# Layer 1's modulation products: 16 of 32 move from layer 0's output projection to its second attention's keys and queries

## The chip, the cores and the metric

The kernel runs on one core of one Trainium2 chip. Its time is device microseconds of one execution, the median of several runs. A core has TensorE (PE: matrix products), VectorE (DVE), ScalarE (ACT) and GpSimd (POOL) for work on tiles, and SyncE (SP), whose queue here issues most DMAs. All engines run side by side; each takes its own instructions in order, and semaphores tie them together.

## The reference, cut to what matters

Two layers of a transformer trunk with two attention branches, for 512 latent and 256 context tokens of width 1024. Layer 1 computes latent tokens alone. Everything is float32 at the borders.

```python
def _layer(x, ctx, c, c_ctx, w_ada, b_ada, norm_g, w_in, ..., update_ctx):
    mod_x = jax.nn.silu(c) @ w_ada + b_ada                 # (3 * 1024,)
    shift_x, scale_x, gate_x = jnp.split(mod_x[:, None, :], 3, axis=-1)
    mod_c = jax.nn.silu(c_ctx) @ w_ada + b_ada
    shift_c, scale_c, gate_c = jnp.split(mod_c, 3)
    hx = _rmsnorm(x, norm_g) * (1.0 + scale_x) + shift_x
    hc = _rmsnorm(ctx, norm_g) * (1.0 + scale_c) + shift_c
    px = hx @ w_in                                         # keys, values, queries, z paths, gates
    ...
    a_att = _na_latent(qa, ka, va, cka, cva, rpb, rows)    # first attention: a 2-D window and all context
    b_att = _gqa_latent(qb, k_all, v_all)                  # second attention: 8 query heads, 2 key/value heads
    o_a = (a_att * jax.nn.silu(a_z)) @ w_o_a
    o_b = (b_att * jax.nn.silu(b_z)) @ w_o_b
    out_x = (jax.nn.sigmoid(g_a) * o_a + jax.nn.sigmoid(g_b) * o_b) @ w_out
    x_new = x + gate_x * out_x
```

The vectors `c` and `c_ctx` are known from the start, so the modulation of both layers can be computed at any time before it is used: layer 1's shift and scale are first used when its normalised rows are made, at the end of layer 0.

## The kernel before, in words

**Products on TensorE.** Each float32 product is made of three: operands are split into a high and a low half (`whi` by ScalarE, `wlo` by VectorE or GpSimd), and high x high, high x low and low x high are summed in PSUM (`mm3`, lines 435 to 437). `tok_proj` projects one tile of 128 tokens with all eight blocks of the contracted dimension; `chan_proj` projects one block of 128 output channels.

**The modulation.** Layer 0's shift and scale are products on TensorE at the start. The rest is computed on VectorE in the background: `ada_steps` gives a list of steps, to be run one by one between the pieces of other work. For one half `h` of the contracted dimension (512 of 1024), a first step (`load`, line 286) broadcasts that half of silu(c) and silu(c_ctx) to all partitions, a tile `cb` with a single buffer. Then there are, for each of the named blocks `i` of 128 output channels, two products (`dot`, line 297), one for c and one for c_ctx: a multiply-sum along 512 elements on VectorE. The first of the two also issues the load of the block's weights (`rawb`, 256 KB, line 290, two buffers), on SP's queue or on another that is named. `asum` keeps the sums, and `ada_mod(1)` makes layer 1's shift and scale (`modc`) of both halves. Blocks 0 to 15 are shift and scale, 16 to 23 the gate. `gate_steps` is the same for the gate of the layer itself.

Each product is tied by `behind(ON_DVE, ...)` to stand after the VectorE instruction that was emitted last. Otherwise a planner (the tile framework's scheduler) orders every engine's instructions before the run, in program order where its own estimate says that they are ready, and ahead of it where they are ready earlier.

**The stages of layer 0, with their background lists.**

- First value projection: layer 1's first half, blocks 0 to 15, both vectors.
- First attention (window).
- Second attention's keys and values (`load_w2(W, C_BKV, ...)`, six token tiles, lines 1110 to 1114), then its queries (six token tiles, lines 1126 to 1133): the list is `gate_steps((0,))`, 17 steps, one a tile and then two a tile. In each tile `head_rstd` sums squares (line 505, VectorE; 508, GpSimd), `rope_heads` scales and rotates (lines 517, 586, 591 on VectorE, 588 on GpSimd, the last two for latent tokens only), and `turn` transposes on TensorE (line 529), two tiles later (`hp["lag"]`). After the last tile, two pieces of the gate projection are run with the last transposes behind them, and the heads' pool is closed.
- Second attention: `gate_steps((1,))` and the rest of the gate projections and the first branch's output projection (`fill`) in the background. `prepare` splits the first branch's result in halves, with four subtractions on GpSimd (line 668).
- Merge and output projection (`w_out`, lines 1242 to 1266, two halves of the output channels with six token tiles each): the list is layer 1's second half, its weights loaded by GpSimd's queue (`G`), and `ada_mod(1)`. It is spread over the six tiles of the first half:

```python
            bg = ada_steps(1, range(16), (1,), 2, mp, G) + [lambda: ada_mod(1)] if first else []
            run(bg, 1)
            per_bg = -(-len(bg) // nt)
```

  In the second half each finished tile goes through `make_hx` (a sum of squares on ScalarE, line 330, GpSimd's power, 331 and 332, and the scaled row `y` on VectorE, 334) and `turn_hx` (transposes on TensorE, line 343, shift and scale on ScalarE, 346) into layer 1's input.

Of the kernel before, what the change touches and what calls it, by code (L numbers as in the profile page):

```python
# [52 lines left out]
def R(ap):  # L53
    return ap.bitcast(F32R)
# [18 lines left out]
def hybrid_kernel(es: ExitStack, tc, x, ctx, cvec, w_ada, w_ada0, small, gvec, w_in, w_o_a, w_o_b, w_out,  # L73
                  bias_int, bias_edge, rope, ident_d, out):
    nc = tc.nc
    V, S, G, T = nc.vector, nc.scalar, nc.gpsimd, nc.tensor
# [10 lines left out]
    def nm(s):  # L87
        uid[0] += 1
        return f"{s}_{uid[0]}"
# [188 lines left out]
    def ada_steps(l, tiles, halves, nv, pool, queue=None):  # L278

        cb = {}  # L280

        def load(h):
            cb[h] = pool.tile([128, 2, 512], F32, tag="cb", name=nm("cb"), bufs=1)
            for v in range(nv):
                src = cd[8 * v + 4 * h:8 * v + 4 * h + 4].rearrange("k p -> (k p)").unsqueeze(0)
                nc.sync.dma_start(cb[h][:, v, :], src.to_broadcast([128, 512]))

        def load_tile(h, i):
            cb["w"] = pool.tile([128, 512], F32, tag="rawb", name=nm("rawb"), bufs=2)
            (queue or nc.sync).dma_start(cb["w"], w_ada[l, h, i])  # L290

        def dot(h, i, v):
            if v == 0:
                load_tile(h, i)
            w = cb["w"]
            o = w if v == nv - 1 else pool.tile([128, 512], BF16, tag="junk", name=nm("junk"), bufs=1)
            behind(ON_DVE, lambda: V.tensor_tensor_reduce(o, w, cb[h][:, v, :], 1.0, 0.0, ALU.mult, ALU.add,
                                                          asum[:, i, h, v:v + 1]))
        res = []
        for h in halves:  # L300
            res += [lambda h=h: load(h)] + [lambda h=h, i=i, v=v: dot(h, i, v) for i in tiles for v in range(nv)]
        return res

    def ada_sum(a, b, nv):
        s = sp.tile([128, b - a, 2], F32, tag="as", name=nm("as"), bufs=1)
        V.tensor_tensor(s[:, :, 0:nv], asum[:, a:b, 0, 0:nv], asum[:, a:b, 1, 0:nv], ALU.add)
        return s

    def ada_mod(l):
        mod_finish(l, ada_sum(0, 16, 2).rearrange("p (a k) v -> p a k v", a=2), 0, 8)  # L310
# [157 lines left out]
    hp = {"late": [], "lag": 0}  # L468
# [4 lines left out]
    def behind(engine, fn, after=None):  # L473

        n = len(nc.cur_bb.bb.instructions)
        after = latest(engine, 1) if after is None else after
        fn()
        for i in nc.cur_bb.bb.instructions[n:]:
            if i.engine == engine:
                for last in after:  # L480
                    tc.add_manual_dep(i, last, mybir.DependencyInfo(
                        mybir.DependencyClass.NoSync, mybir.DependencyReason.DATA), reason="program order")
                after = [i.name]
# [6 lines left out]
    def run(fill, n):  # L490
        for _ in range(min(n, len(fill))):
            fill.pop(0)()
# [102 lines left out]
    def layer(l, hx, nxt, start):  # L595
        first = l == 0
# [7 lines left out]
        def gate_steps(halves, pool):  # L604
            return (ada_steps(l, range(16, 24), halves, nv, pool)
                    + ([lambda: ada_gate(l, nv, pool)] if 1 in halves else []))
# [100 lines left out]
        if first:  # L707
# [22 lines left out]
            bg = ada_steps(1, range(16), (0,), 2, hp["p"])  # L730
        else:
# [5 lines left out]
            bg = gate_steps((0, 1), hp["p"])  # L737
# [49 lines left out]
        if True:  # L787
# [267 lines left out]
            bg = []  # L1055
# [40 lines left out]
                halves(vf.rearrange("p t (h d) -> p (t h) d", h=2), vb.rearrange("p t h q d -> p (t h) q d"),  # L1096
                       vs[:, 0:1])

            bg = gate_steps((0,), hp["p"]) if first else []
            w = load_w2(W, C_BKV, KT, mix_lo)  # L1100
            w_q = []

# [7 lines left out]
            for t in range(6):  # L1110
                tok_proj(w, 256, a_hx, t, evac_bkv)
                if t == 2:
                    behind(ON_DVE, lambda: make_tabs(0))
                run(bg, 1)
            hp["lag"] = 2
            qbv = big("qb").rearrange("p (j n) -> p j n", j=4)
            fill = in_order(gates[n_na:] + o_chunks("a", prepare, evac_a))
# [7 lines left out]
                    rope_heads(4, ps, rs, gbc[:, 0, :], None, qbv, t)  # L1125
            for t in range(qt):
                tok_proj(w_q, 512, a_hx, t, evac_bq)
                run(bg, 2)
                if t == STAGE_T[0]:
                    split_vb()  # L1130
                if t in STAGE_T:
                    e = STAGE_T.index(t)
                    stage_k(kbv[:, 0, :], e, gkt[e][0], gkt[e][1], True)
# [66 lines left out]
            bg = gate_steps((1,), Parts(att["p"], own)) if first else []  # L1200
# [3 lines left out]
        with tc.tile_pool(name=f"mrg{l}", bufs=1, reuse_waits="tile") as mp:  # L1204
            open_ps(x=5)
            extra = lambda name: mp.tile([128, 3072], F32, tag="extra", name=nm(name))
            gv = mp.tile([128, nv, DM], F32, tag="gate", name=nm("gate"), bufs=1)
            for v in range(nv):
                src = gd[l][8 * v:8 * v + 8].rearrange("k p -> (k p)").unsqueeze(0)
                nc.sync.dma_start(gv[:, v, :], src.to_broadcast([128, DM]))  # L1210
            hilo(zb, gated["b"], [3], V, spans)
            mg = []

            def evac_b(f, n0, n1, ps):
                a, b = tg_part(0, f, n0, n1), tg_part(1, f, n0, n1)
                V.scalar_tensor_tensor(b, b, 1.0, ps, ALU.add, ALU.mult)  # L1216
                V.tensor_tensor(a, a, b, ALU.add)  # L1217
                hi, lo = [m[:, f % 4, n0:n1] for m in mg[f // 4]]
                S.copy(R(hi), a)
                V.tensor_tensor(R(lo), a, hi, ALU.subtract)  # L1220
            chunks = o_chunks("b", None, evac_b)
            chunks[0][0]()
            for i in range(4):
                if i < 3:
                    chunks[i + 1][0]()
                if i % 2 == 0:
                    mg.append(hilo_tiles("m"))
                for piece in chunks[i][1]:
                    piece()

            nt = 6 if first else 4
            xv = [a.rearrange("p (t n) -> p t n", t=3) for a in (big("xt0"), extra("xt1"))]
            xts = []
            for t in range(nt):
                xt = xv[t // 3][:, t % 3, :]
                nc.sync.dma_start(xt, x_src(t) if first else xs1[128 * t:128 * t + 128, :])
                xts.append(xt)
            a_m = lambda part, k: mg[k // 4][part][:, k % 4, :]
            bg = ada_steps(1, range(16), (1,), 2, mp, G) + [lambda: ada_mod(1)] if first else []
            run(bg, 1)  # L1240
            per_bg = -(-len(bg) // nt)
            for n in range(2):
                w = load_w(w_out[l], 512 * n, 512, KT, mix_lo)

                def evac_o(t, ps, n=n):
                    cs = slice(512 * n, 512 * n + 512)
                    t1 = mp.tile([128, 512], F32, tag="t1", name=nm("t1"), bufs=2)
                    V.tensor_tensor(t1, ps, gv[:, 0 if t < 4 else 1, cs], ALU.mult)
                    xt = xts[t]
                    V.tensor_tensor(xt[:, cs], xt[:, cs], t1, ALU.add)  # L1250
                    if not first:
                        nc.sync.dma_start(o_lat[16 * t:16 * t + 16][:, :, cs], xt[:, cs])
                    elif n == 1:
                        if t < 4:
                            G.dma_start(xs1[128 * t:128 * t + 128, :], xt)
                        late.append(lambda: make_hx(1, t, xt, nxt(), mp))
                late = []
                if first and n == 1:
                    hp["lag"] = 2
                for t in range(nt):  # L1260
                    if not first and n == 1 and t == nt - 1:
                        break
                    tok_proj(w, 512, a_m, t, evac_o)
                    run(bg, per_bg)
                    run(late, len(late))
                turn_late(0)
            if not first:

                for c0, c1 in ((0, 256), (256, 512)):
                    ws = [(hi[:, c0:c1], lo[:, c0:c1]) for hi, lo in w]  # L1270
                    cs = slice(512 + c0, 512 + c1)
                    ps = psw(c1 - c0)
                    tok_mm(ps, ws, c1 - c0, a_m, nt - 1, 0, KT)
                    t1 = mp.tile([128, 512], F32, tag="t1", name=nm("t1"), bufs=2)[:, :c1 - c0]
                    V.tensor_tensor(t1, ps, gv[:, 0, cs], ALU.mult)
                    xt = xts[nt - 1]
                    V.tensor_tensor(xt[:, cs], xt[:, cs], t1, ALU.add)
                    (nc.sync if c0 else S).dma_start(o_lat[16 * nt - 16:16 * nt][:, :, cs], xt[:, cs])
# [247 lines left out]
```

## Time and profile before

| what | value |
|---|---|
| time, median of 3 runs | 1110.77 us (1109.96 to 1110.95) |
| the profiled execution's own time | 1110.55 us |
| its span, first to last instruction | 1108.8 us |
| mean granted TensorE clock | 0.995 |
| keys, values and queries of layer 0's second attention | about 300 to 360 us |
| layer 0's second attention | about 374 to 545 us |
| layer 0's output projection | about 585 to 650 us |

In the profile's rows a line number is that of the instruction's source line, which is often a helper's. PE stands for TensorE's matrix products, PEld for its weight loads, SPq for SyncE's queue of DMAs. Ends of matrix products are modelled, so PE's busy time is an upper bound.

### The profile page before, as it was taken

The numbers are of one execution on the slowest core, as the hardware profiler recorded it, in microseconds if no ns is written. First come the engines' busy times: TensorE is split into PE (matmuls) and PEld (weight loads), VectorE is DVE, ScalarE is ACT, GpSimd is POOL, SyncE is SP. The second block draws the span as 40 slices with busy tenths as digits, with TensorE's granted clock in tenths as the row PEclk, the third lists the DMA queues.
The fourth block names the chain that finished last, engine by engine and source line by source line (L and its number), as shares of the span: only waits on it lengthen the run. The fifth ranks groups of instructions, "written<-read, shape, count | busy, mean of one in ns | idle before, by whom it ended". The sixth has DMA issues, their size and how long they took to land. (4 is left out here: it accounts for less than half of the span.)

```text
span 1108.8 us, 16943 instructions
## 1 busy us (share of the span) xinstructions
PE 1074.5 (97%) x5672; PEld 876.9 (79%) x5672; DVE 767.4 (69%) x1600; ACT 617.2 (56%) x1236; POOL 470.1 (42%) x397
## 2 busy tenths in 40 slices
PE   8999999899999999979999999999999999999998
PEld 6688888788888877757788878888877888777677
DVE  5567799974378478676577785466997665777473
ACT  6464279776333566655330275444899446786430
POOL 1044235554256244454521455232355472564531
PEclk9999999999999999989999999999999999999999
DMA  9454325554543498769533542453565536879642
GB/s 374 153 169 143 91 70 116 125 137 121 174 141 117 132 205 185 172 185 271 171 105 125 166 136 82 138 165 99 132 148 130 156 106 171 200 232 236 188 152 77
DMA packets 236001, 171.79 MB, mean 155 GB/s; under 512 B 160141, under 2 KB 201865, under 8 KB 234249
## 3 DMA queue, kind: packets, MB, share of 16 engines
q1 hardware_dynamic: 228576, 156.31, 51.7%
q0 software_dynamic: 2368, 7.87, 2.2%
q10 hardware_dynamic: 4968, 6.53, 1.8%
q8 instruction: 45, 0.74, 0.3%
q14 instruction: 44, 0.35, 0.1%
HBM read 115.58 MB, written 17.32 MB: 120 GB/s over the span
## 5 line engine op out<-in xcount | busy, mean ns | idle before, releaser
L838 POOL TENSOR_TENSOR h<-p,h 128x256 f16<-128x256 f32 (+2 forms) x104 | 113.1, 1096 | 167.7 <-ACT h L837 119.9
L422 POOL TENSOR_TENSOR wlo<-raw,whi 128x512 fp32r<-128x512 f32 x70 | 98.8, 1416 | 124.5 <-ACT whi L420 80.9
L435 PE MATMUL psf<-hx,whi 128*128 128x512 f32 (+1 forms) x360 | 137.5, 382 | 2.5 <-ACT zt L625 1.3
L437 PE MATMUL psf<-hx,wlo 128*128 128x512 f32 (+1 forms) x360 | 135.5, 376 | 0.0
L436 PE MATMUL psf<-hx,whi 128*128 128x512 f32 (+1 forms) x360 | 135.4, 376 | 0.0
L435 PE MATMUL psx<-whi,hx 128*128 128x512 f32 (+1 forms) x328 | 121.0, 372 | 0.0
L420 ACT CAST whi<-raw 128x512 fp32r<-128x512 f32 x136 | 82.9, 620 | 67.5 <-DMA raw<-in_w_in_dram 48.3
L437 PE MATMUL psx<-whi,hx 128*128 128x512 f32 (+1 forms) x328 | 120.0, 367 | 0.0
L436 PE MATMUL psx<-wlo,hx 128*128 128x512 f32 (+1 forms) x328 | 119.6, 366 | 0.0
L408 POOL TENSOR_TENSOR wlo<-raw,whi 128x512 fp32r<-128x512 f32 x40 | 59.5, 1489 | 119.2 <-ACT whi L405 76.0
L405 ACT CAST whi<-raw 128x512 fp32r<-128x512 f32 x88 | 54.2, 623 | 96.8 <-PE psx L437 34.2
L508 POOL TENSOR_TENSOR ss<-ss,ehalf 128x8 f32<-128x8 f32 (+2 forms) x40 | 63.6, 1593 | 77.8 <-DVE ss L505 72.5
L422 DVE TENSOR_TENSOR wlo<-raw,whi 128x512 fp32r<-128x512 f32 x66 | 70.8, 1073 | 35.2 <-ACT whi L420 34.1
L837 ACT CAST h<-p 128x256 f16<-128x256 f32 (+2 forms) x136 | 81.6, 616 | 7.7 <-DMA ct<-h 3.7
L435 PEld LDWEIGHTS psf<-hx,whi 128*128 128x128 f32 x360 | 67.8, 188 | 15.1 <-ACT zt L625 2.5
L1157 DVE CUSTOM_DVE_ANT_0 p<-pss,vb 128x768 f32<-128x768 f32 x64 | 60.4, 954 | 25.4 <-PE pss L887 22.7
L1158 ACT ACTIVATE p<-pss,mx 128x768 f32<-128x768 f32 x64 | 57.6, 901 | 35.7 <-DVE mx L1157 34.8
L437 PEld LDWEIGHTS psf<-hx,wlo 128*128 128x128 f32 x360 | 67.8, 188 | 11.8
L436 PEld LDWEIGHTS psf<-hx,whi 128*128 128x128 f32 x360 | 67.9, 189 | 10.7
L437 PEld LDWEIGHTS psx<-whi,hx 128*128 128x128 f32 x328 | 61.9, 189 | 10.2
L436 PEld LDWEIGHTS psx<-wlo,hx 128*128 128x128 f32 x328 | 62.0, 189 | 9.4
L435 PEld LDWEIGHTS psx<-whi,hx 128*128 128x128 f32 x328 | 61.8, 189 | 9.1 <-issue 0.2
(338 smaller groups left out, 2972.4 us busy)
## 6 DMA issues: line engine op xcount, KB each, us to landing
raw<-in_w_in_dram SPq DMA_DIRECT2D x168, 256.0 KB, 2.9
rawb<-in_w_ada_dram SPq DMA_DIRECT2D x48, 256.0 KB, 2.8
raw<-in_w_out_dram SPq DMA_DIRECT2D x32, 256.0 KB, 2.9
tg<-gs SPq DMA_DIRECT2D x4, 1536.0 KB, 7.1
rawx<-in_w_ada_dram SPq DMA_DIRECT2D x4, 1024.0 KB, 10.7
rawy<-in_w_ada_dram SPq DMA_DIRECT2D x4, 1024.0 KB, 9.3
gs<-zt ACTq DMA_DIRECT2D x16, 256.0 KB, 2.9
raw<-in_w_o_a_dram SPq DMA_DIRECT2D x16, 256.0 KB, 3.1
```

The source lines that it names most:

```text
L405: S.copy(hi[:, :n], raw[:, :n])
L408: e.tensor_tensor(lo[:, :n], raw[:, :n], F(hi[:, :n]), ALU.subtract)
L420: S.copy(hi, raw)
L422: lo_eng(i).tensor_tensor(lo, raw, F(hi), ALU.subtract)
L435: T.matmul(ps, lhs[0], rhs[0], start=first, stop=False)
L436: T.matmul(ps, lhs[0], rhs[1], start=False, stop=False)
L437: T.matmul(ps, lhs[1], rhs[0], start=False, stop=last)
L508: G.tensor_tensor(ss, ss, ehalf[:, :n], ALU.pow)
L837: S.copy(h[:, 0], p[:, :n])
L838: eng.tensor_tensor(h[:, 1], p[:, :n], h[:, 0], ALU.subtract)
L1157: V.tensor_tensor_reduce(p, pss, lift, -1.0, 3e38, ALU.add, ALU.min, mx[:, 0:1])
L1158: S.activation(p, pss, AF.Exp, bias=mx[:, 0:1], accum_out=r[:, i:i + 1])
```

## The change

The steps of layer 1's second half are cut in two lists. Blocks 0 to 7, 16 products behind a broadcast of their own, are put behind the gate's steps in the list of the second attention's keys and queries, and that list is run at twice the pace. Their weights are loaded by SP's queue. Blocks 8 to 15 and `ada_mod(1)` stay in the output projection.

```diff
-            bg = gate_steps((0,), hp["p"]) if first else []
+            bg = gate_steps((0,), hp["p"]) + ada_steps(1, range(8), (1,), 2, hp["p"]) if first else []
             w = load_w2(W, C_BKV, KT, mix_lo)
...
                 tok_proj(w, 256, a_hx, t, evac_bkv)
                 if t == 2:
                     behind(ON_DVE, lambda: make_tabs(0))
-                run(bg, 1)
+                run(bg, 2)
...
                 tok_proj(w_q, 512, a_hx, t, evac_bq)
-                run(bg, 2)
+                run(bg, 4)
...
-            bg = ada_steps(1, range(16), (1,), 2, mp, G) + [lambda: ada_mod(1)] if first else []
+            bg = ada_steps(1, range(8, 16), (1,), 2, mp, G) + [lambda: ada_mod(1)] if first else []
```

In layer 1 both lists are empty, so nothing changes there in the program.

## The prediction

> **What bounds the kernel now.** I read the page first (engine shares, slices, costly groups), then the table by stretches for the two stages that the change touches, then who waited for whom there, and last the instructions in order of time around each wait. The page's first row names the bound:
>
> ```profile
> PE 1074.5 (97%) x5672; PEld 876.9 (79%) x5672; DVE 767.4 (69%) x1600; ACT 617.2 (56%) x1236; POOL 470.1 (42%) x397
> ```
>
> Time can be won or lost only where TensorE (PE) stands still, or where its clock is not full. The table by stretches (us, then PE, PEld, DVE, ACT, POOL busy with counts, clock, DMA share, GB/s) for the second attention's keys and queries of layer 0 (300 to 360) and its output projection (585 to 645):
>
> ```profile
> 300.00:360.00 60.00, 60.00 (x349) 52.21 (x348) 44.71 (x92) 23.43 (x49) 35.08 (x27) 1.00 0.43 137
> 585.00:645.00 60.00, 58.62 (x263) 48.10 (x262) 45.09 (x103) 11.92 (x24) 19.81 (x28) 1.00 0.49 157
> 90.00:150.00 60.00, 60.00 (x302) 49.97 (x301) 48.69 (x107) 25.43 (x40) 19.05 (x11) 1.00 0.33 101
> ```
>
> PE has no idle time at all in the first and 1.4 us in the second. The third row, layer 0's first value projection, carries 32 such products and is the fullest VectorE stretch: 48.7 of 60 us, without a PE gap. The products themselves (line 297), by the same table for these instructions alone; the count holds two instructions a product, the multiply-sum and the read of its accumulator:
>
> ```profile
> 300.00:360.00 60.00, 12.24 (x30) 1.00 0.43 137
> 585.00:645.00 60.00, 22.05 (x64) 1.00 0.49 157
> ```
>
> So 15 products in the keys-and-queries stretch cost 0.82 us each, and 32 in the output projection 0.69. The difference is waiting for GpSimd (below).
>
> **What the output projection gives up, and gets.** 16 of 32 products leave, 16 x 0.69 = 11.0 us of VectorE, with 8 of 16 loads of 256 KB from POOL's queue. The only PE wait there is for the first transpose of layer 1's normalised rows (the products' group, min/median/max ns, first and last start; then rows in order of time, us, duration, in brackets the idle time before and what ended it):
>
> ```profile
> L297 DVE CUSTOM_DVE_ANT_0 junk<-rawb,cb x16: 674/688/694, 593.9 to 637.8; 128x512 bf16<-128x512 f32 x16
> ...
> 633.09 0.69 DVE L1248 TENSOR_TENSOR t<-psx,gate 128x512 f32<-128x512 f32 x1
> 633.69 0.68 DVE L297 CUSTOM_DVE_ANT_0 rawb<-rawb,cb 128x512 f32<-128x512 f32 x1
> 634.30 0.69 DVE L1250 TENSOR_TENSOR xt<-xt,t 128x512 f32<-128x512 f32 x1
> ...
> 637.82 0.69 DVE L297 CUSTOM_DVE_ANT_0 junk<-rawb,cb 128x512 bf16<-128x512 f32 x1 [0.41 <-DMA rawb<-in_w_ada_dram]
> 638.43 0.76 DVE L334 TENSOR_SCALAR y<-xt,ss 128x1024 f32<-128x1024 f32 x1
> 639.71 0.67 DVE L297 CUSTOM_DVE_ANT_0 rawb<-rawb,cb 128x512 f32<-128x512 f32 x1
> ...
> 639.25 1.09 PE L343 MATMUL pst<-ident,y 128*128 128x128 f32 x8 [1.38 <-DVE y L334]
> ```
>
> Products stand inside this chain: one between the two steps of the residual (0.61 us from start to start), one ahead of y (0.61). The first product starts at 593.9 and the last at 639.7: 16 tiles in 46 us, 2.9 each, paced by a load that waits for the products two tiles back. Eight tiles end near 593.9 + 23 = 617, so none is left at 633. The chain comes 1.2 us earlier, and the wait for a load in front of 637.82 goes too (0.4): the 1.38 us wait is gone. **Gain 1.4 us** (0 to 1.4: there is no other idle PE time in the stage). Next in line nothing is late: the modulation is ready near 620, its first reader ran at 642.8, and it feeds a PE that is busy for 20 of 20 us:
>
> ```profile
> 642.80 2.89 ACT L346 ACTIVATE half<-pst,modc 128x128 f32<-128x128 f32 x8
> 645.00:665.00 20.00, 20.00 (x104) 16.62 (x103) 17.25 (x27) 16.67 (x41) 9.70 (x11) 1.00 0.39 119
> ```
>
> POOL loses 8 issues and the waits before them; the one PE wait in 585 to 645 is not for POOL: 0.
>
> **What the keys and queries take on.** The background list grows from 17 places (a broadcast load and 16 gate products) to 34, taken two a token tile in the key/value loop and four in the query loop instead of one and two: 12 places, then 4, 4, 4, 4, 4, 2. The added broadcast is the 18th place, in the second query tile, so the 16 moved products fall into the last four and a half query tiles, and the gate products are pressed ahead of them. Added VectorE time by that stretch's own price: 16 x 0.82 = 13.1 us. The stretch would stand at 44.7 + 13.1 = 57.8 of 60, far above the fullest that runs without a PE gap (48.7).
>
> Its 15.3 idle us are not free, since most are links of the chain that makes each query tile (VectorE's waits, 290 to 375: us in total, times, longest):
>
> ```profile
> DVE ry L517 <- POOL ss L508: 8.4, 8, 1.8
> DVE rr L591 <- POOL ry L588: 2.6, 5, 1.2
> ```
>
> A product fits into such a gap only when the order of VectorE's queue puts it there; it is tied behind the last VectorE step emitted, so products of a tile lie ahead of the next tile's sum of squares. I take half of the idle time, 7.6 us, as filled. One more product than before lies behind the last tile's chain (0.8). So the last tile's rotated queries come 13.1 - 0.8 - 7.6 = 4.7 us late. How much slack they have stands in the order of time:
>
> ```profile
> 346.05 1.78 DVE L297 CUSTOM_DVE_ANT_0 rawb<-rawb,cb 128x512 f32<-128x512 f32 x1
> 347.76 1.77 DVE L297 CUSTOM_DVE_ANT_0 junk<-rawb,cb 128x512 bf16<-128x512 f32 x1
> ...
> 347.24 1.75 POOL L422 TENSOR_TENSOR wlo<-raw,whi 128x512 fp32r<-128x512 f32 x1
> ...
> 359.63 0.69 DVE L586 TENSOR_TENSOR rr<-ry,gbc 128x512 f32<-128x512 f32 x1
> 360.46 0.63 PE L529 MATMUL pst<-ident,rr 128*128 128x128 f32 x4
> 362.62 1.94 DVE L880 TENSOR_TENSOR qs<-qb,qs 64x768 fp32r<-64x768 f32 x2 [1.69 <-ACT qs L879]
> 374.08 0.40 PE L886 MATMUL pss<-gk,qs 128*128 128x512 f32 x1
> ```
>
> The queries are done at 360.32 and transposed at 360.46: slack 0.14. PE takes its queue in order, so a delay is a PE wait unless the planner, which fixed the order beforehand, puts the next gate projection ahead (24 matmuls at 58.62/263 = 0.22, 5.4 us). With that the stall is 0: after it the scores have cover, 374.08 - 364.56 = 9.5 us. **Stall 0 to 4.6 us; I take 4.0**, near the upper end, because the transposes now stand at the earliest place the program allows, and a planner does not see what waiting on GpSimd adds.
>
> That waiting is in the rows: two products took 1.78 us instead of 0.69 while GpSimd split a weight. [...] By the old place's price (0.69) the delay would be 11.0 - 0.7 - 7.6 = 2.7 us.
>
> **Queues and loads.** SP issues eight more tile loads in place of POOL, and two more broadcasts:
>
> ```profile
> rawb<-in_w_ada_dram SPq DMA_DIRECT2D x48, 256.0 KB, 2.8
> rawb<-in_w_ada_dram POOLq DMA_DIRECT2D x16, 256.0 KB, 3.1
> cb<-cd SPq DMA_DIRECT2D x8, 256.0 KB, 4.8
> SPq L290 <- DVE asum L297: 28.3, 5, 9.5
> 355.80 0.68 DVE L422 TENSOR_TENSOR wlo<-raw,whi 128x512 fp32r<-128x512 f32 x1
> 360.85 0.48 PE L435 MATMUL psx<-hx,whi 128*128 128x512 f32 x1
> ```
>
> A tile load on SP waits for the products two tiles back (9.5 us at the longest), and gate weights are queued behind it. Their last low halves are made at 355.8 and read by the projection that starts at 360.9, with k in order: some 6 us of cover. I take 0; if the cover is gone, the price is 9.5 - 6 = 3.5 us. The added broadcast has one buffer: its load waits for the last gate product, then 4.8 us to land. Behind the first moved product on VectorE lie the next tile's sum of squares and, through it, PE's transposes. Bounds 0 (the next tile's steps are ordered first) to 4.8; I take 0, since a planner that knows the load's length orders ready steps first. The bytes are moved, not added, except 0.5 MB at a DMA share of 0.43: 0. The two products of the last tile end before 374 either way: 0.
>
> **Sum.** 4.0 - 1.4 = +2.6 us. The profiled execution took 1110.55 us, 1108.8 of span and 1.75 around it, 0.22 under the median. So 1113.15 for such an execution and **1113.4** against the median of 1110.77. The case's own range: 1110.8 - 1.4 + 0 = 1109.4 to 1110.8 - 1.4 + 4.6 + 3.5 = 1117.5. The 3.5 also holds what a fall of the clock after a stall would cost (1.7, worked out below); the 1.38 us wait brought none. A measurement of this kernel can tell about 0.2%, 2.2 us, from no change.
>
> **Rivals.**
> *Faster: a blocked split in the attention falls elsewhere.* The dearest place between the two stages:
>
> ```profile
> 483.66 8.22 DVE L422 TENSOR_TENSOR wlo<-raw,whi 128x512 fp32r<-128x512 f32 x1
> 482.98 7.12 POOL L668 TENSOR_TENSOR gal<-za,gah 128x768 fp32r<-128x768 f32 x4
> PE psv L849 <- DVE ho L825: 5.8, 1, 5.8
> 490.00:495.00 5.00, 1.44 (x5) 1.25 (x6) 4.10 (x6) 0.00 (x0) 2.74 (x4) 0.65 0.53 109
> 495.00:500.00 5.00, 5.00 (x19) 3.75 (x18) 3.44 (x5) 1.82 (x3) 0.79 (x2) 0.66 0.55 130
> ```
>
> A split that takes 0.69 us when free begins 0.7 us into GpSimd's run of four subtractions and ends 1.8 us after it. PE waits 5.8 us, and the clock falls to half: about 0.35 x 10 = 3.5 us at half speed there, of which half, 1.7, is lost. The moved products change the order that the planner carries into the attention; if the split begins 3 us later or earlier than the run, 3 to 5.8 us of wait and the 1.7 go. With the stall in the queries at 1.5: 1.5 - 1.4 - 5.0 = -4.9, so 1105.9. For it: a run of 7 us on GpSimd with this much lost occurs once in the trace, so another order is likelier to meet it better than worse. Against: the four subtractions stay one run, and the attention's own list is not edited.
> *Same: the gaps hold all.* The stall is 0 to 1: 1109.4 to 1110.4. For it: PE now has no wait in this stretch. Against: 57.8 of 60.
> *Slower still:* SP holds the gate weights back: 2.6 + 3.5 = +6.1, 1116.9; decided where a weight load lands after 360.
> *The change does not do what it says:* the planner lets the moved products drift behind the queries, into the stretch of 361 to 374: no stall, 1109.4 to 1110.8.
>
> **Chances.** Forecast (stall of 1 to 4.6, more with the clock) 0.45: 0.37 with a stall over 3.6, which is slower by over 2.2 us, and 0.08 within. Faster rival 0.33. Same 0.10. Slower still 0.08. Not as said 0.04, half of it within 0.2% and half faster. Sums: faster 0.35, within 0.2% 0.20, slower 0.45. Range 1103.5 to 1117.5: below the faster rival by 2.4 for its full price, up to the forecast's own end; some 2 in 10 stay outside. Cases of both signs hold most of the chance, so the forecast's own range is the 1109.4 to 1117.5 above.
>
> **What would show it.** Right: PE waits at line 529 on VectorE's line 586 near 360 to 366, 2 to 5 us in all; VectorE over 54 of 60 us in that stretch; no wait at line 343; last product of the output projection near 617 to 621. Wrong: PE without a gap from 300 to 374; a wait at line 343 as before; or a difference that lies mostly between 380 and 545, where line 422's 8.22 us would be found shorter, or another split as long.

## The result, and the profile after

| | before | after |
|---|---|---|
| median of 5 runs each, side by side | 1110.77 us (1109.96 to 1112.39) | 1117.14 us (1116.51 to 1118.36) |
| the profiled execution's own time | 1110.55 us | 1116.51 us |
| its span | 1108.8 us | 1114.6 us |

The ratio is 1.0054, with a 95% interval of 1.0043 to 1.0065: the change makes the kernel slower by about 6 us. The forecast was 1113.4 us with a range up to 1117.5, so the sign was right and the size was at the far end. (A ratio here is an estimate over all runs and can differ by 0.1% from that of the two medians.)

The table by stretches of the kernel after, for the two stages (us, then PE, PEld, DVE, ACT, POOL busy with counts, clock, DMA share, GB/s):

```profile
300.00:360.00 60.00, 59.01 (x338) 50.85 (x337) 49.99 (x111) 22.33 (x48) 33.99 (x26) 1.00 0.53 163
585.00:645.00 60.00, 60.00 (x276) 50.00 (x275) 42.31 (x83) 14.08 (x25) 15.17 (x20) 1.00 0.42 136
```

The output projection has no idle PE time left (58.62 of 60 before). The keys and queries, which had none, lost 1.0 us before 360, and the greater part just behind it. PE's waits between 300 and 380 (us in total, times, longest); before had none here:

```profile
PE pst L529 <- DVE rr L586: 3.4, 1, 3.4
PE pst L529 <- DVE rr L591: 1.0, 1, 1.0
```

The order of time around the longer one shows what made it. VectorE, then the transposes on PE:

```profile
347.06 0.69 DVE L297 CUSTOM_DVE_ANT_0 junk<-rawb,cb 128x512 bf16<-128x512 f32 x1 [1.03 <-DMA cb<-cd]
...
360.19 0.68 DVE L505 TENSOR_REDUCE ss<-sq 128x8 f32<-128x520 f32 x1
361.34 0.69 DVE L297 CUSTOM_DVE_ANT_0 junk<-rawb,cb 128x512 bf16<-128x512 f32 x1 [0.47 <-DMA rawb<-in_w_ada_dram]
...
364.61 0.69 DVE L297 CUSTOM_DVE_ANT_0 junk<-rawb,cb 128x512 bf16<-128x512 f32 x1 [1.83 <-DMA rawb<-in_w_ada_dram]
...
365.22 0.69 DVE L517 TENSOR_TENSOR ry<-psx,ss 128x512 f32<-128x512 f32 x1
...
366.43 0.69 DVE L586 TENSOR_TENSOR rr<-ry,gbc 128x512 f32<-128x512 f32 x1
...
367.27 0.63 PE L529 MATMUL pst<-ident,rr 128*128 128x128 f32 x4 [3.44 <-DVE rr L586]
...
381.58 0.40 PE L886 MATMUL pss<-gk,qs 128*128 128x512 f32 x1
```

Between the last query tile's sum of squares (360.19) and its scaling at line 517 (365.22) stand three moved products, and two of them wait for their weights, 0.47 and 1.83 us. Line 586 starts at 366.43, where before it started at 359.63: 6.8 us late. Of this, 1.0 us has nothing to do with the stage: its first transposes (line 529) already start at 310.69 against 309.70, and PE has been that much late since 164 us, long before the first moved product. The kernel of experiment 8, which is that of before up to the attention, is 1.5 us late there, so executions differ by as much without any moved product. The stage itself makes line 586 late by 5.8 us. PE had put four matmuls of the gate projection ahead and then stood for 3.44 us. After the stall the clock fell. It changes at 368.64 and at 372.05, 3.41 us apart; the two stretches before are laid off with the same length:

```profile
361.81:365.23 3.42, 2.02 (x14) 1.49 (x12) 1.55 (x7) 0.38 (x1) 0.84 (x1) 1.00 0.85 277
365.23:368.64 3.41, 1.37 (x8) 1.25 (x9) 3.20 (x10) 0.68 (x2) 0.00 (x0) 1.00 0.08 26
368.64:372.05 3.41, 3.41 (x9) 2.67 (x8) 1.91 (x2) 1.57 (x2) 0.00 (x0) 0.50 0.48 154
```

In the third, the granted clock is 0.50 for 3.41 us, which by estimate (half of that time) costs 1.7 us. The first score of the attention starts at 381.58 in place of 374.08, 7.5 us late: 1.0 from ahead of the stage, 4.4 of waits, 1.7 of clock, and 0.4 that no single row carries. At the end of the attention it is 8.2 (the last transposes of line 1174 start at 545.91 against 537.72; the wait at line 849 is 6.9 us in place of 5.8). From the output projection on 2.2 us come back, of which 1.4 is the wait at line 343, and the end is 6.0 late.

### The profile page after: what moved, and what is told of

Read it like the earlier page. It is cut to its first block, busy times and chain, and to the rows that moved or that the text cites. A ratio compares the mean times of both kernels' runs of the same rounds, so it can differ in the third digit from the quotient of the medians.

```text
span 1114.6 us, 16948 instructions
## 1 busy us (share of the span) xinstructions
PE 1075.0 (96%) x5672; PEld 876.7 (79%) x5672; DVE 771.0 (69%) x1600; ACT 616.5 (55%) x1236; POOL 463.8 (42%) x389
```

## The experiments

In every batch the kernel before ran beside them: medians of 1111.16 us (29 runs) for the first four, 1111.03 (23) for the next four, 1111.14 (17) for the last four. The change itself has the ratio 1.0054; the ratios below are to the kernel before as well.

**1. The relief alone.** The 16 products of blocks 0 to 7 are left out, and their sums are set to zero.

```diff
-            bg = ada_steps(1, range(16), (1,), 2, mp, G) + ...
+            bg = ada_steps(1, range(8, 16), (1,), 2, mp, G) + ...     # in the output projection only
```

> The output projection's part alone: the 16 products of blocks 0 to 7 are left out (their sums are set to zero), the keys and queries are as before. If the two parts add up as the traces say, the 1.4 us wait at line 343 is gone and nothing else moves: 1.4 to 1.8 us under before, about 1109.2. Rival (the relief is worth nothing, since PE is full there anyway): within 0.5 us of before. Rival (the gain is larger, some 3 us, since layer 1 starts earlier too): 1107.5.

1109.58 us, ratio 0.9989 (0.9978 to 1.0000). The stage from 585 to 645 has no idle PE time; the keys and queries have none either, as before:

```profile
585.00:645.00 60.00, 60.00 (x275) 49.77 (x274) 39.14 (x77) 15.56 (x32) 15.30 (x22) 1.00 0.40 132
```

The gain, 1.2 us by the ratio (0 to 2.4), agrees with the wait of 1.4; the interval can't tell more.

**2. The added products alone.** All 32 products stay in the output projection as well.

```diff
-            bg = ada_steps(1, range(8, 16), (1,), 2, mp, G) + ...
+            bg = ada_steps(1, range(16), (1,), 2, mp, G) + ...        # keys and queries as in the change
```

> The other part alone: the 16 products run in the keys and queries as in the change, and all 32 run in the output projection again (16 of them twice, to the same sums). If the parts add up: the waits at line 529 (3.4 and 1.0 us) and the clock's fall as in the change, the 1.4 us wait at line 343 as in before, so 1.4 to 1.8 us over the change, about 1118.7. Rival (part of the loss comes from the changed output projection): not over the change, 1117 or less.

1119.59 us, ratio 1.0076 (1.0061 to 1.0091), +8.4 us. PE's waits:

```profile
PE pst L529 <- DVE rr L586: 3.9, 1, 3.9
PE pst L529 <- DVE rr L591: 1.8, 1, 1.8
...
PE pst L343 <- DVE y L334: 0.7, 1, 0.7
```

The clock falls behind them as in the change (mean 0.84 from 365 to 370 and 0.82 from 370 to 375, which would be 3.4 us at 0.50). +8.4 and -1.6 make +6.8, near the +6.4 of the change: within the noise the two parts add up, and the loss sits in the keys and queries. The waits at line 529 are 5.7 us, where the same edit left 4.4 in the change, so the rows agree less closely than the times; the wait at line 343 is 0.7 us, where 1.4 had been expected.

**3. The last transposes later.** The last query tile is turned behind one more piece of the gate projection, so that PE has work while VectorE is late.

```diff
-                turn_late(1 if i == 0 else 0)
+                turn_late((1, 1, 0, 0)[i] if first else 1 if i == 0 else 0)
```

> The change, with the last query tile's transposes put one piece of the gate projection later in PE's order (behind the third piece instead of the second). Theory (PE waits in order for the last tile's queries, which VectorE makes late): the 3.4 us wait at line 529 goes below 0.5, the clock does not fall, the scores still have cover, so 4 to 5.5 us under the change, about 1112.3. Rival (the delay of the queries only moves on to the scores): the wait appears before the first scores, within 1 us of the change. Rival (the loss lies in the attention's changed order): within 1 us of the change, without a wait there.

1113.68 us, ratio 1.0023 (1.0011 to 1.0034): 3.4 us of the loss went, less than the 4 to 5.5 expected. The wait on line 586 is gone and with it the fall of the clock (1.00 from 365 to 375), though VectorE does the same work. Part of the gain was lost again later:

```profile
PE pst L1174 <- DMA ht<-h: 1.9, 1, 1.9
PE pst L529 <- DVE rr L591: 1.0, 1, 1.0
...
PE psv L849 <- DVE r L847: 7.6, 1, 7.6
PE pss L886 <- ACT p L905: 4.9, 2, 3.5
```

The wait at line 886 was 1.3 us in the kernel before and in the change, that at line 849 5.8 and 6.9. That PE stands in order behind the late queries was thus a cause, and an order that avoids this wait has a price of its own.

**4. One load for all moved products.** The same work on VectorE, with one weight load in place of eight. (The second product of a block then writes to a scratch tile, since the weights are read again.)

```diff
-            if v == 0:
+            if v == 0 and not (once and "w" in cb):
                 load_tile(h, i)
```

> The change, but the 16 moved products all read the first block's weights: one load of 256 KB instead of eight (so seven blocks' sums are not the reference's). Theory (VectorE's time): the waits of products for their loads (0.2, 0.5 and 1.8 us in the trace) go, so the last transposes wait 1 to 2 us instead of 3.4, and the total is 2 to 4 us under the change, 1113 to 1115. Rival (the loads alone are the cause): no wait at line 529, 5.5 us or more under the change, 1111.6 or less. Rival (the loads cost nothing): within 1 us of the change.

1113.03 us, ratio 1.0026 (1.0013 to 1.0038). VectorE's waits for weights are gone (that for the broadcast, 1.2 us, stays), and the stall on line 586 is halved; the fall of the clock is gone with it (1.00 from 350 to 375):

```profile
PE pst L529 <- DVE rr L586: 1.7, 1, 1.7
PE pst L529 <- DVE rr L591: 1.0, 1, 1.0
```

**5. The products behind the queries.** The list keeps the pace of before, and the moved products follow the gate pieces behind the last tile, four behind each.

```diff
-                run(bg, 2)        # key/value loop, 4 in the query loop
+                run(bg, 1)        # 2 in the query loop, and 4 behind each of the four gate pieces
```

> The change with the 16 moved products put behind the last query tile: the two loops keep the pace of before (one and two places a tile), and four products follow each of the four pieces of the gate projection, where VectorE was busy 5.7 of 16 us. Theory: nothing stands ahead of the last tile's queries, so no wait at line 529, and the output projection's relief is kept: 1.2 to 1.6 us under before, 1109.5. Rival (the queries' pool, which is closed behind the products, gives its memory to the attention too late): a wait before the first scores, 1 to 4 us over before.

1116.06 us, ratio 1.0048 (1.0035 to 1.0061); 1109.5 had been expected. No wait at line 529 is left, but VectorE waits in front of its first, and the attention's queries (line 880) stand behind its last:

```profile
366.48 0.69 DVE L297 CUSTOM_DVE_ANT_0 junk<-rawb,cb 128x512 bf16<-128x512 f32 x1 [3.59 <-DMA cb<-cd]
...
385.01 0.69 DVE L297 CUSTOM_DVE_ANT_0 junk<-rawb,cb 128x512 bf16<-128x512 f32 x1 [2.77 <-DMA rawb<-in_w_ada_dram]
...
386.48 1.94 DVE L880 TENSOR_TENSOR qs<-qb,qs 64x768 fp32r<-64x768 f32 x2
...
PE pss L886 <- DVE qs L880: 2.5, 1, 2.5
```

VectorE has room behind the queries, but the products there need 20 us, since four of their eight loads come late. The wait had only changed its place. Later in the attention the mean clock is 0.75 from 435 to 440 and 0.91 from 440 to 445, where the kernel before has 1.00.

**6. An even pace.** Three places a tile in both loops.

```diff
-                run(bg, 2)        # key/value loop
+                run(bg, 3)
-                run(bg, 4)        # query loop
+                run(bg, 3)
```

> The change with three places a tile in both loops: all gate products and the broadcast in the key/value tiles, then 3, 3, 3, 3, 3, 1 moved products. As many products stand ahead of the last query tile's chain as in the change (31 against 30), but the broadcast and the loads come earlier and VectorE's key/value gaps are used. Theory (VectorE's time, with load waits on top): the load waits go, the last transposes wait 1 to 2 us, the clock stays: 1113 to 1115. Rival (only the number of products counts): within 1 us of the change, 1117.

1114.76 us, ratio 1.0032 (1.0020 to 1.0044). The same work, now ending earlier, leaves 3.2 us of waits in four pieces, and no fall of the clock (1.00 from 350 to 375):

```profile
PE pst L529 <- DVE rr L586: 1.6, 2, 1.3
PE pst L529 <- DVE rr L591: 1.6, 2, 1.1
```

Its profiled execution took 1112.34 us, 2.4 under its median, so these rows account for a part of the loss alone.

**7. Short products.** The moved products multiply 64 of 512 elements; loads and broadcast stay.

```diff
-            ... V.tensor_tensor_reduce(o, w, cb[h][:, v, :], ...
+            ... V.tensor_tensor_reduce(o[:, :n], w[:, :n], cb[h][:, v, :n], ...      # n=64
```

> The change, but each of the 16 moved products works on 64 of its 512 elements (so these sums are not the reference's); all loads stay. VectorE is relieved of some 16 x 0.5 = 8 us, the loads are not. Theory (VectorE's time makes the delay, and the waits for loads add to it only because there is no slack): no wait over 0.5 us at line 529, 1109.5 to 1111. Rival (waits for loads alone suffice): a wait of 1.5 us or more stays at line 529, 1112 or more.

1113.51 us, ratio 1.0013 (1.0000 to 1.0026), against 1109.5 to 1111 expected. VectorE is busy for 46.59 of the 60 us in place of 49.99, and yet 2.0 us of waits stay, with longer waits for loads. The time is in the range that its rival had named (waits for loads alone suffice, 1112 or more):

```profile
PE pst L529 <- DVE rr L586: 1.1, 1, 1.1
PE pst L529 <- DVE rr L591: 0.9, 1, 0.9
...
DVE junk L297 <- DMA rawb<-in_w_ada_dram: 5.0, 3, 2.6
```

Experiments 4 and 7 belong together. Without the weight loads 2.7 of 4.4 us stay; with a third of the work (0.22 us a product in place of 0.69) 2.0 stay, though the products' waits for weights and broadcast grew from 3.5 to 7.0 us. So both count and neither alone explains the stall; how it divides between them isn't settled, since taking from the one changed the other.

**8. The attention's run of four, split.** This one is made from the kernel before, and tests the price that stood in the faster rival: two of GpSimd's four subtractions (line 668) go to VectorE.

```diff
-            hilo(za, gated["a"], range(4))
+            for f in range(4):
+                hilo(za, gated["a"], (f,), V if f % 2 else G)
```

> The kernel before, with two of the four subtractions of the first branch's halves (line 668, in prepare) on VectorE instead of GpSimd, so that GpSimd's run of four is cut. This prices the place that the faster rival spoke of. If VectorE's blocked weight split is what PE waits for: no VectorE instruction over 4 us near 484, PE's wait of 5.8 us at line 849 mostly gone and no half clock: 5 to 7.5 us under before, 1103.5 to 1106. Rival (the wait has another cause, VectorE's own work there): within 2 us of before.

1122.31 us, ratio 1.0090 (1.0076 to 1.0104): slower by 11 us where 5 to 7 faster had been expected. The long split at line 422 is gone (0.68 us in place of 8.22); a 2-element step took 4.78 us instead, beside GpSimd's split and its two remaining subtractions (483.12 to 488.71), and PE's waits moved to other places:

```profile
483.96 4.78 DVE L902 TENSOR_SCALAR mx<-mx 128x2 f32<-128x2 f32 x1
...
PE psf L435 <- DVE tg L704: 5.7, 4, 3.7
```

The edit holds in layer 1 as well, where PE waits 3.9 us for line 704 (0.7 for line 703 before), and PE's waits from 560 to 700 are 4.4 us in place of 1.4. Not all of the 11 us are accounted for by rows. What it shows is that the rival's price (the wait and the clock) isn't to be had by breaking up that run in this way.

**9. Half the products.** Blocks 0 to 3 move; three places a tile in the query loop.

```diff
-  ada_steps(1, range(8), (1,), 2, hp["p"])     ...  ada_steps(1, range(8, 16), (1,), 2, mp, G)
+  ada_steps(1, range(4), (1,), 2, hp["p"])     ...  ada_steps(1, range(4, 16), (1,), 2, mp, G)
```

> Only blocks 0 to 3 move: 8 products in place of 16 go to the keys and queries (query loop at 3 places a tile), 24 stay in the output projection. My theory: relief needs only that the last product there ends before 633; 12 tiles at 2.9 us from 593.9 end near 629, so the wait at line 343 is gone and -1.2 to -1.6 us stand. VectorE in 300 to 360 stands near 44.7 + 8 x 0.82 = 51.3; the list ends a tile before the last, so the last tile's queries are late by at most 1 us: waits at line 529 of 0 to 1 us, no fall of the clock near 368. Time 1109.5 to 1110.8. Rival, the price is by the product: half of 7.0 us, 3.5, and with the relief 1112.5 to 1113.

1115.23 us, ratio 1.0042 (1.0028 to 1.0056): a miss. Half of the work keeps most of the loss, by another wait. VectorE, PE, and two stretches of 3.41 us:

```profile
348.95 0.69 DVE L297 CUSTOM_DVE_ANT_0 junk<-rawb,cb 128x512 bf16<-128x512 f32 x1 [2.30 <-DMA cb<-cd]
...
353.67 1.73 DVE L591 TENSOR_TENSOR rr<-rr,ry 128x512 f32<-128x512 f32 x1 [0.87 <-POOL ry L588]
...
355.55 0.63 PE L529 MATMUL pst<-ident,rr 128*128 128x128 f32 x4 [2.03 <-DVE rr L591]
...
352.89:356.30 3.41, 1.38 (x9) 0.92 (x8) 2.63 (x4) 0.00 (x0) 3.41 (x3) 1.00 0.08 11
356.30:359.71 3.41, 3.41 (x10) 2.64 (x9) 3.38 (x7) 1.59 (x3) 2.08 (x2) 0.50 0.76 214
```

The first moved product waits 2.30 us for the added broadcast, and two tiles' queries stand behind it. One of them comes 2.0 us late, and the clock falls after that: 2.0 + 1.7 = 3.7 us. The wait at line 343 is gone here too (-1.4), which leaves 2.3 of the measured 4.1; in its profile 1.3 more stands ahead of the stage (311.03 against 309.70). Line 591 also took 1.73 us in place of 0.69 and waited 0.87 for GpSimd, so the broadcast is not all of the 2.0.

**10. Even pace and later transposes together.** The edits of experiments 3 and 6.

> The change with three places a tile in both loops and the last tile's transposes one gate piece later. My theory: the two edits work on the same wait, so they don't add up: the even pace alone left 3.2 us at line 529, of which the later turn covers what stands at the last tile (about 1.6), and the later first scores cost some of it again. Time 1112 to 1114; waits at line 529 under 2 us. Rival, the two add: 1117.1 - 2.4 - 3.5 = 1111.2 or less.

1115.41 us, ratio 1.0035 (1.0021 to 1.0049), over the 1112 to 1114 expected. The waits at line 529 are down to 1.8 us, and those of the later order in the attention are there again:

```profile
PE pst L529 <- DVE rr L591: 1.4, 2, 0.9
PE pst L529 <- DVE rr L586: 0.4, 1, 0.4
...
PE psv L849 <- DVE r L847: 7.0, 1, 7.0
PE pss L886 <- ACT p L905: 3.5, 1, 3.5
```

**11. The moved loads on GpSimd's queue.** All 16 products move; only the queue of their eight loads is another.

```diff
-            bg = gate_steps((0,), hp["p"]) + ada_steps(1, range(8), (1,), 2, hp["p"]) if first else []
+            bg = gate_steps((0,), hp["p"]) + ada_steps(1, range(8), (1,), 2, hp["p"], G) if first else []
```

> The change with the moved products' eight weight loads issued by GpSimd's queue in place of SyncE's. If SyncE's queue (gate weights and other loads ahead, held) is what makes the moved products wait, VectorE's waits for rawb near 361 to 365 (0.5 and 1.8 us) are gone and the stall at line 529 falls from 4.4 to about 2.5, near 1113.5. If it is the two buffers (a load starts only when the products two tiles back are done, then about 2.9 us), the waits stay and the time is that of the change, 1116.5 to 1118. Third: GpSimd stands behind its own issues, which wait for buffers, and its sums of squares (line 508) come later: waits at line 517 and 529 grow, 1118 to 1122.

1111.18 us, ratio 1.0003 (0.9991 to 1.0014): as fast as before, and better than any of the three theories had it. VectorE's row for the broadcast, its last query steps and the waits behind them, and PE's waits:

```profile
346.32 0.69 DVE L297 CUSTOM_DVE_ANT_0 junk<-rawb,cb 128x512 bf16<-128x512 f32 x1 [0.28 <-DMA cb<-cd]
...
358.34 0.68 DVE L505 TENSOR_REDUCE ss<-sq 128x8 f32<-128x520 f32 x1
...
361.60 0.69 DVE L517 TENSOR_TENSOR ry<-psx,ss 128x512 f32<-128x512 f32 x1
...
362.81 0.69 DVE L586 TENSOR_TENSOR rr<-ry,gbc 128x512 f32<-128x512 f32 x1
...
365.32 0.69 DVE L297 CUSTOM_DVE_ANT_0 junk<-rawb,cb 128x512 bf16<-128x512 f32 x1 [1.22 <-DMA rawb<-in_w_ada_dram]
...
PE pst L529 <- DVE rr L586: 0.9, 1, 0.9
```

VectorE still waits for weights, 2.1 us in all against 2.5 in the change, so these waits come with either queue, as the second theory (two buffers) has it; its time did not come. Line 586 starts 3.6 us earlier than in the change (362.81 against 366.43). 1.9 of them are there at the last tile's sum of squares (358.34 against 360.19): the wait for the broadcast is shorter, and the planner put this step ahead of line 586 of the tile before, and not behind it. The other 1.8 lie between that sum and line 517: two products stand there in place of three, and the wait of 1.22 us comes behind the last queries, where nothing hangs on it. The stall is 0.9 us in place of 4.4, and the clock doesn't fall (1.00 from 350 to 375): 5.2 us of the change's 6. GpSimd waits in front of its issues (6.5 us in all), and its sums of squares were not later for it (line 517 waits for them 3.3 us in all, 3.2 in the change). Why the planner chose this order, and what the order alone would give with the loads on SP, was not tried apart.

**12. Half the products and later transposes.** The edits of experiments 9 and 3.

> Only blocks 0 to 3 move, and the last tile's transposes stand one gate piece later. If half the products leave no wait at line 529, the later turn only brings the first scores later: 0 to 1.5 us over the kernel with half the products alone, 1110 to 1112. If a wait is left there, the later turn takes it away: 1109.3 to 1110.3.

1115.62 us, ratio 1.0038 (1.0024 to 1.0052), where 1109.3 to 1112 had been expected. The wait on line 591 (2.0 us) is that of experiment 9, ahead of the edit, and the attention's waits are those of experiment 3. No version that does all the work beat the kernel before.

## Why the prediction was right or wrong

**Relief, 1.4 us: right.** The wait at line 343 is gone, in the change and in experiment 1. The last of the 16 products that stay starts at 627.6; with the stage itself 8 us later, that is the foretold 617 to 621.

**The stall in the keys and queries: right in place and size, wrong in its working.** 4.4 us of waits at line 529, on lines 586 and 591, stand against 4.0 (0 to 4.6). The planner did put other work ahead, but four matmuls, 0.9 us, in place of all 24. The sum behind the 4.0 was made differently by the chip. VectorE was not filled to 57.8 us but to 49.99, since the products and the last tile spilled past 360; the mark of over 54 us, named as a sign of being right, did not come. Its waits between 300 and 375 show what the idle time became:

```profile
DVE ry L517 <- POOL ss L508: 3.2, 4, 1.8
DVE junk L297 <- DMA rawb<-in_w_ada_dram: 2.5, 3, 1.8
DVE rr L591 <- POOL ry L588: 2.0, 5, 0.8
DVE junk L297 <- DMA cb<-cd: 1.0, 1, 1.0
```

The two old waits gave up 5.8 us (8.4 to 3.2, and 2.6 to 2.0), and smaller ones 1.4. But 3.5 us of new waits, for weights and broadcast, came in, and I had none of them in the sum. So VectorE's idle time up to line 586 fell by 3.7 us, half of the 7.6 that I took as filled. Its work up to there grew by less, too: from 44.34 us (300 to 359.63 before) to 53.81 (300.99 to 366.43 after), 9.5 in place of 13.1 - 0.8 = 12.3. The two errors have opposite signs: 5.8 us late in the stage, where I had 4.7. That the stall came so near to 4.0 is in part luck.

**The added broadcast, taken at 0: the step that failed with the loads.** VectorE waited 1.0 us for it, and 1.0 of the stall is most likely its price: the wait on line 591 was 1.0, 1.8, 2.0 and nothing where the wait for the broadcast was 1.03, 1.8, 2.30 and 0.28 (change, experiments 2, 9 and 11). It is not shown apart, and line 591 can be late without it: in experiment 6, where VectorE does not wait for the broadcast, PE waits 1.6 us there. The planner did not order the next tile's steps first.

**The loads on SP: looked for on the wrong side.** I priced gate weights held back behind the new loads; no wait for them came, so 0 was right there. The cost was on the other side of the same queue: the products' own loads came late, with VectorE's order fixed behind them.

**The clock, kept in the range alone: the term that was mis-sized most.** By the estimate above it cost 1.7 us, in the change and in experiment 9. The forecast's 1.7 is the right figure by luck: it took a mean clock of 0.65 over 10 us as 3.5 us at half clock, but in that trace the clock is 0.50 for 6.83 us (491.52 to 498.35). With 4.4 and 1.7 for the 4.0, less 1.4, the sum would have been +4.7; of the measured +6.0 in the two profiled executions, 1.0 stands ahead of the stage, and 0.3 is left as the balance of small differences.

**The faster rival fell.** Line 422 took as long as before in the change (8.22 us at the longest), and the wait behind it was a little longer:

```profile
L422 DVE TENSOR_TENSOR wlo<-raw,whi x66: 662/693/8217, 96.1 to 1042.5; 128x512 fp32r<-128x512 f32 x66
PE psv L849 <- DVE ho L825: 6.9, 1, 6.9
```

The same wait stands in all the runs of experiments 1 to 7 and 9 to 12, at 5.6 to 7.6 us: no order upstream that was tried here loosened it. The *same* rival fell as well for this change, and came nearly true in experiment 11, with other loads (a stall of 0.9 us, 1111.18). *Slower still* gave about the right time (1116.9) by the wrong mechanism. The products did not drift behind the queries: two of the 16 stand behind the last line 586.

## What to carry to other kernels

A product that is put in an engine's idle time brings its loads' waits with it (3.5 us here). In VectorE's order two of them stood in front of the last query tile's scaling (0.47 and 1.83 us), so ask for each moved step where its operand lands, and what stands behind it, before counting its busy time. An engine at 50 of 60 us can hold up another that has no slack: what counted here was whether the last tile's two steps stood ahead of a waiting product or behind it (4.4 against 0.9 us, with the same work; only the loads' queue was edited, and VectorE's order came out differently with it). Halving the load did not halve the price (4.1 us in experiment 9, 6.4 in the change). And before two traces are compared, look for the lag that stands ahead of the changed stage: here 1.0 us of 6.0.

## What the runs showed of the hardware

**When the clock falls.** Behind the stalls of the change and of experiment 9 the clock was at 0.50 for 3.41 us; in the attention it was so for 6.83 us in both profiled kernels (491.52 to 498.35 before, 498.35 to 505.17 after). With 1.37 and 1.38 us of PE's busy time in 3.41 us the next 3.41 us were at 0.50 (the change and experiment 9, above). The 3.41 us before that in the change had 2.02 and were followed by full clock. In experiment 5 a wait of 2.5 us, longer than the 2.0 of experiment 9, cost no clock. The rows around it:

```profile
382.89:386.30 3.41, 2.10 (x10) 1.41 (x8) 1.25 (x3) 0.00 (x0) 0.00 (x0) 1.00 0.26 91
386.30:389.71 3.41, 1.89 (x9) 1.40 (x9) 3.28 (x7) 1.51 (x3) 0.00 (x0) 1.00 0.61 181
389.71:393.13 3.42, 3.07 (x25) 3.07 (x26) 1.70 (x5) 3.39 (x8) 0.00 (x0) 1.00 0.24 87
```

So two stalls here, of 2.0 and 3.4 us, cost 1.7 us more by the estimate above, and one of 2.5 us cost nothing more: its length alone does not tell. What decides it was not shown.

**A short step that took long.** In experiment 8 VectorE's TENSOR_SCALAR on 128 x 2 elements took 4.78 us beside GpSimd's split and subtractions, and ended with them (488.74 and 488.71). In the kernel before the eight steps of this line (901 there) take 0.13 to 1.42 us, 0.18 at the median. Why this one took so long, no run here shows.
